# Neighbourhood attention with query tiles moved by half a block, one-bank score tiles and one transposed tile

## The chip, the cores and the metric

One core of a Trainium2 chip runs the whole program. The metric is device time in microseconds, from the runs of the program on that core; lower is better. Line numbers (L2205) are those of the kernel before.

## The reference, cut to what matters

The program is a stack of four transformer layers on 512 tokens. The last of them mixes tokens by neighbourhood attention, and only that layer is concerned here. The 512 latent tokens form a grid of 8 rows and 64 columns; 256 context tokens are keys as well. A query in column c sees all 8 rows of the 16 columns from clip(c - 8, 0, 48) on, and all 256 context keys:

```python
q, k, v, z = split(u @ w_in)           # 32 heads of 64; q and k are normalised
win_start = clip(cols - 8, 0, 48)
s = q . k_band * scale + rpb[row difference, column difference]
s = where(win_start <= kc < win_start + 16, s, -inf)
p = softmax(concat([s, q . k_ctx * scale]))
out = (p_band @ v_band + p_ctx @ v_ctx) * silu(z) @ w_out
```

## The kernel before, in words

Tokens are stored column by column (`grid_order`), 8 rows to a column, so 128 tokens are 16 grid columns and a query sees 128 consecutive keys. The layer (`second`, L1620, with L = 3) works in eight groups of four heads. While the attention of group g runs, the projections of group g+1 (q, k, v) and the gate z of group g are computed beside it as *pieces*, 24 matmuls each, which a table (`fill`) puts into numbered steps. Matrix products are made in two parts: each operand is a high part (fp32r) and a remainder, so a product is three matmuls (`mm3`, L583 to L585); the weights are split by ScalarE (L277) and GpSimd (L278) from a buffer that SP loads (L264).

`na_run` (L2168) runs 128 units, one for each group, head h and query tile j of 128 tokens. Latent keys come in four blocks of 128. Tile j needs the blocks B0[j] to B0[j]+NB[j]-1, that is two blocks for the outer tiles (j = 0, 3) and three for the middle ones (j = 1, 2), and the two blocks of the context. A unit goes through these functions:

- `A` (L2194): scores in PSUM tile `s` of two banks, of which there is **one** (`s.psum(3, 3, 0, 1)`, L1919): 256 or 384 latent columns and 256 context columns, each with KH and with KL (L2205, L2206). Rows 64 to 127 of KH and KL are copies of rows 0 to 63 made by a transfer on GpSimd's queue (`dup_now`, L1803). For j = 1, `bias` loads the next head's position bias (192 KB, L2190, on SP) and GpSimd adds it to three masks (L2192).
- `B` (L2208): VectorE adds mask and bias and takes the row maximum in one pass (L2221).
- `E` (L2224): ScalarE's exponential out of PSUM into P with the row sum.
- `Dm` (L2228): VectorE scales P by the reciprocal of the sum (L2231, L2232).
- `T` (L2234): TensorE transposes P's blocks (L2244) into two PSUM tiles, latent and context; ScalarE copies each as the high part (`pth`, `pch`; L411), VectorE subtracts for the remainder (`ptl`, `pcl`; L414).
- `G` (L2248), once per head: values times the transposed probabilities, four matmuls of 512 columns for the context (L2253) and two for each latent block over the two or three query tiles that see it (L2259). ScalarE moves half of the result (L2261), VectorE adds the other (L2262).
- `Y` (L2264): GpSimd multiplies by the gate, SP stores.

The order in a step i is written out by hand at the end of `na_run` (L2271 on): scores of unit i, deferred work (`s.due`), the first half of the step's piece, B of unit i, G if a head is complete, T of unit i-1, E of unit i, the rest of the piece, further pieces, Dm of unit i. Each engine runs its instructions in that order. `stack` (L1775) transposes the projected q and k and writes QS (high part in rows 0 to 63, remainder in rows 64 to 127) and KH, KL; its remainders are deferred by a step (`low`).

Of the kernel before, what the change touches and what calls it, by code (L numbers as in the profile page):

```python
# [161 lines left out]
def pack_cst():  # L162
# [11 lines left out]
    cols = np.arange(64)  # L174
    ws = np.clip(cols - 8, 0, 48)
    na = []
    for cb, b0, nb in ((0, 0, 2), (1, 0, 3), (3, 2, 2)):
        qc = cb * 16 + np.arange(128) // 8
        kc = b0 * 16 + np.arange(nb * 128) // 8
        ok = (kc[None, :] >= ws[qc][:, None]) & (kc[None, :] < ws[qc][:, None] + 16)  # L180
        na.append(np.where(ok, 0.0, NEG))
# [8 lines left out]
             ("cos", tok(cos)), ("sin", tok(sin * sgn)), ("mask", mask), ("na", np.concatenate(na, axis=1))]  # L190
    o = 0
# [11 lines left out]
def pack_rpb(i):  # L203
    rpb = i["b_rpb_2"][0]
    q = np.arange(128)
    qc, r = q // 8, q % 8
    k = np.arange(384)
    kc, kr = k // 8 - 16, k % 8
    a = kr[None, :] - r[:, None] + 7
    b = np.clip(kc[None, :] - qc[:, None] + 15, 0, 30)  # L210
    return np.ascontiguousarray(rpb[:, a, b])
# [89 lines left out]
class Next:  # L301
    """Normalised input of a layer, feature-major in two parts, filled a pair of token tiles at a time."""
# [76 lines left out]
class Net:  # L379
# [207 lines left out]
    def tm(s, ps, units, xh, xl, tok, n, ks=range(8)):  # L587
        """Eight blocks of a token-major product, or those of ks."""
# [6 lines left out]
    def fmm(s, ps, units, xh, xl, tok, n, c0=0, m=128, ks=range(8)):  # L595
        """The same with the features on the partitions."""
# [14 lines left out]
    def rows_gemm(s, keys, lhs, evac, tail, npair, flush, wide_first=False, mid=None, k_first=False):  # L611
        """Token-major product over four 256-column chunks; the last two go pair of tiles by pair of tiles."""
# [23 lines left out]
        def pair(i, c, us, free, between):  # L636
            """Two tiles, one weight unit after the other; the first unit is given back early where it is free."""
# [69 lines left out]
    def causal(s, units, qk, scale, mask, vs, pt, out, P, tmp, ofs, wide, fill, extra=lambda t: None):  # L707
        """Causal attention over (head, query tile) units; fill[t] holds the pieces of other work run in step t."""
# [368 lines left out]
    def out_proj(s, name, order, lhs, M, ssp, rowt, sqp, make, gain, part=None, late=None):  # L1077
        """part: the first chunk's sum over the first unit, already formed."""
# [502 lines left out]
    def tables2(s, pool, tmp):  # L1581
        """Rotary tables with the head gains folded in, the difference's factor and the output gain."""
# [37 lines left out]
    def second(s, L, nx):  # L1620
# [20 lines left out]
        QS = gp.tile([128, 4, qw], F32R, name="QS")  # L1641
# [114 lines left out]
        def gates_at(ts, g, chunks):  # L1756
            """z / (1 + exp(-z)), 128 columns at a time."""
# [17 lines left out]
        def stack(n, pr, tiles):  # L1775
            gain = None if diff else s.p("b" + n)
            c = slice(tiles[0] * 128, tiles[-1] * 128 + 128)
# [9 lines left out]
            def low():  # L1787
                for t in range(2):
# [130 lines left out]
        s.psum(*(2, 2, 0, 2) if diff else (3, 3, 0, 1))  # L1919
# [248 lines left out]
    def na_run(s, c):  # L2168
        nc, io, X = s.nc, s.io, s.X
        QS, KH, KL, SZ, V, yd = c.QS, c.KH, c.KL, c.SZ, c.V, c.yd  # L2170
        gp = s.pool("nag")
        na = gp.tile([128, 896], F32, name="na")
# [3 lines left out]
        WO = ((0, 512, 256), (1536, 1152, 1792))  # L2176
        pth, ptl = [gp.tile([128, 12, 128], F32R, name=n) for n in ("pth", "ptl")]
        pch, pcl = [gp.tile([128, 2, 512], F32R, name=n) for n in ("pch", "pcl")]
        B0 = (0, 0, 1, 2)
        NB = (2, 3, 3, 2)  # L2180
        rpb = X[0][:, 640:1024]
        P = [X[0][:, :640], X[1][:, :640]]
# [4 lines left out]
        def bias(h):  # L2187
            if h > 31:
                return
            nc.sync.dma_start(rpb, io["rpb"][h])  # L2190
            for o, a, c, w in zip(WO[h % 2], (128, 0, 0), (0, 256, 640), (256, 384, 256)):
                nc.gpsimd.tensor_tensor(bm[:, o:o + w], na[:, c:c + w], rpb[:, a:a + w], OP.add)  # L2192

        def A(u):  # L2194
# [3 lines left out]
            ps = s.s2.tile([128, 1024], F32, name="s2")  # L2198
            q = QS[:, h, j * 128:(j + 1) * 128]
            w = NB[j] * 128  # L2200
            k0 = B0[j] * 128
            c = 256 if h % 2 else 512
            x = d[u] = {"s": ps[:, 256:512 + w] if h % 2 else ps[:, 512 - w:768]}
            for o, kk in ((ps[:, 512:512 + w] if h % 2 else ps[:, 512 - w:512], slice(k0, k0 + w)), (ps[:, c:c + 256], slice(512, 768))):
                nc.tensor.matmul(o, q, KH[:, h, kk], start=True, stop=False)  # L2205
                nc.tensor.matmul(o, q, KL[:, h, kk], start=False, stop=True)  # L2206

        def B(u, i):  # L2208
            g, h, j = u
            x = d[u]  # L2210
            S = x["s"]
            w = S.shape[-1]
            o = WO[h % 2][(0, 1, 1, 2)[j]]
            if j in (1, 2):
                t = bm[:, 896:1536] if h % 2 else bm[:, o:o + w]
            else:
                a, b = (896, o) if h % 2 else (o, 896)
                t = bass.AP(tensor=bm.tensor, offset=bm.offset + a, ap=[bm.ap[0], [b - a, 2], [1, 256]])
                S = S.rearrange("p (a b) -> p a b", b=256)
            x["nb"], x["sm"] = [s.sml.tile([128, 1], F32, name=f"na_{k}") for k in ("nb", "s")]  # L2220
            nc.vector.tensor_tensor_reduce(S, S, t, -1.0, 3e38, OP.add, OP.min, x["nb"])  # L2221
            x["P"] = P[i % 2][:, :w]
# [11 lines left out]
        def T(u):  # L2234
            g, h, j = u
            x = d.pop(u)
            n = NB[j]
            b = 2 * B0[j] + j + 1
            sl = slice(b, b + 2 * n - 1, 2)
            q = slice(j * 128, (j + 1) * 128)  # L2240
            for k0, m, H, Lo in ((2 * (h % 2), n, pth[:, sl], ptl[:, sl]), (n * (1 - h % 2), 2, pch[:, :, q], pcl[:, :, q])):
                t = s.tp.tile([128, 4, 128], F32, name="tp")
                for k in range(m):
                    nc.tensor.transpose(t[:, k], x["P"][:, (k0 + k) * 128:(k0 + k + 1) * 128], s.ident)  # L2244
                s.act(H, t[:, :m], AF.Copy)
                s.sub_lo(Lo, t[:, :m], H)

        def G(g, h):  # L2248
            ps = s.mm.tile([128, 512], F32, name="mm")
            VS = V[g]  # L2250
            for k in range(2):
                for w, t in enumerate((pch, pcl)):
                    nc.tensor.matmul(ps, VS[:, 4 + k, h], t[:, k], start=k == 0 and w == 0, stop=False)  # L2253
            for k in range(4):
                c0, c1 = max(0, k - 1), min(3, k + 1)
                b = 2 * k + c0 + 1
                n = c1 - c0 + 1
# [67 lines left out]
```

## Time and profile before

| | |
|---|---|
| three runs | 3265.22, 3266.62, 3267.99 us |
| median | 3266.62 us |
| span of the profiled execution | 3260.0 us |
| instructions | 59267 |
| busy share PE, PEld, DVE, ACT, POOL | 95, 89, 66, 50, 47% |
| stretch of the 128 units | about 2473 to 3192 us of the span |

The profiled execution shows its span, from the first to the last instruction; a run's time has some microseconds around it, here 6.6 to the median. PE is TensorE's matmuls, PEld its weight loads, DVE VectorE, ACT ScalarE, POOL GpSimd, SP the queue of transfers. A matmul's shown duration includes a modelled end that overlaps the next one, so the price of a matmul in a stream is the distance from its start to the next start.

### The profile page before, as it was taken

Reading aid. Unit: us, or ns where it says so; the run is one execution under the profiler, and the core shown is the slowest. Engines: PE = TensorE matmul, PEld = TensorE weight load, DVE = VectorE, ACT = ScalarE, POOL = GpSimd, SP = SyncE. Lnnn points to the kernel's source line nnn. Section 1 sums busy time; section 2 is a strip of 40 time slices with the busy share of each in tenths; the row PEclk is TensorE's granted clock in tenths of the full one; section 3 lists DMA queues with packets and bytes.
Section 4 is the critical chain, followed back from the end, with each engine's and each line's share of the span. In section 5 each row is a group of like instructions: output and inputs, shape, how many; then the busy total and the mean of one; then the engine's idle time right before and its main releaser. Section 6 shows DMA issues by size and latency. Waiting matters only on the chain.

```text
span 3260.0 us, 59267 instructions
## 1 busy us (share of the span) xinstructions
PE 3097.0 (95%) x23124; PEld 2910.2 (89%) x23124; DVE 2143.7 (66%) x4332; ACT 1626.6 (50%) x3923; POOL 1527.3 (47%) x1344
## 2 busy tenths in 40 slices
PE   7999999998899999999999999998999999999889
PEld 7888889887788889889999999988999999999888
DVE  4885434466865354657777777778446777777775
ACT  4544533345765333455555555555235565555552
POOL 3433344434333444474654465443354554545544
PEclk9999999999999999999999999999999999999999
DMA  3122334432123343331222222212422323222324
GB/s 120 59 72 74 108 123 143 136 99 85 36 85 111 123 135 125 116 98 50 63 60 62 61 66 58 69 53 87 152 87 78 88 79 84 78 71 79 90 87 136
DMA packets 91012, 292.30 MB, mean 90 GB/s; under 512 B 18142, under 2 KB 23390, under 8 KB 87660
## 3 DMA queue, kind: packets, MB, share of 16 engines
q1 hardware_dynamic: 84028, 259.33, 24.7%
q0 software_dynamic: 5120, 25.17, 3.6%
q10 hardware_dynamic: 1584, 4.00, 0.4%
q8 instruction: 183, 3.00, 0.4%
q14 instruction: 97, 0.79, 0.1%
HBM read 244.38 MB, written 18.92 MB: 81 GB/s over the span
## 4 chain that ended last, share of the span: by engine, by line
PE 49%; DVE 11%; ACT 5%; issue 4%; POOL 3%; DMA 2%; SPq 0%; POOLq 0%; DVEq 0%; ACTq 0%
PE mm L583 12%; PE mm L585 12%; PE mm L584 12%; PE mm L2102 2%; ACT X L411 2%; POOL w_lo L278 2%; DMA KL<-KL 1%; PE s L2205 1%; PE tp L2244 1%; PE tp L2089 1%; PE mm L2259 1%; DVE s L2052 1%; PE mm L2253 1%; PE s L2206 1%; DVE X L735 1%
## 5 line engine op out<-in xcount | busy, mean ns | idle before, releaser
L278 POOL TENSOR_TENSOR w_lo<-w_raw,w_hi 128x1024 fp32r<-128x1024 f32 (+2 forms) x350 | 880.6, 2520 | 1033.8 <-ACT w_hi L277 1007.8
L583 PE MATMUL mm<-w_hi,hh 128*128 128x256 f32 (+3 forms) x2880 | 836.8, 291 | 7.8 <-ACT w_hi L277 2.5
L584 PE MATMUL mm<-w_lo,hh 128*128 128x256 f32 (+3 forms) x2880 | 817.0, 284 | 11.8 <-POOL w_lo L278 11.7
L585 PE MATMUL mm<-w_hi,hl 128*128 128x256 f32 (+3 forms) x2880 | 818.6, 284 | 2.8 <-POOL hl L414 2.4
L584 PEld LDWEIGHTS mm<-w_lo,hh 128*128 128x128 f32 x2880 | 548.0, 190 | 15.7 <-POOL w_lo L278 14.4
L583 PEld LDWEIGHTS mm<-w_hi,hh 128*128 128x128 f32 x2880 | 547.4, 190 | 16.0 <-ACT df_sq L411 8.5
L585 PEld LDWEIGHTS mm<-w_hi,hl 128*128 128x128 f32 x2880 | 546.2, 190 | 6.4 <-POOL hl L414 5.5
L277 ACT CAST w_hi<-w_raw 128x1024 fp32r<-128x1024 f32 (+2 forms) x355 | 366.5, 1036 | 206.0 <-PE mm L585 171.2
L583 PE MATMUL mm<-hh,w_hi 128*128 128x256 f32 (+1 forms) x1408 | 455.4, 323 | 3.0 <-DVE M L1088 2.8
L584 PE MATMUL mm<-hl,w_hi 128*128 128x256 f32 (+1 forms) x1408 | 448.2, 318 | 0.6
L585 PE MATMUL mm<-hh,w_lo 128*128 128x256 f32 (+1 forms) x1408 | 447.1, 318 | 1.2 <-DVE w_lo L278 1.2
L583 PEld LDWEIGHTS mm<-hh,w_hi 128*128 128x128 f32 x1408 | 266.0, 189 | 29.8 <-issue 5.2
L584 PE MATMUL mm<-w_lo,gh 128*128 128x256 f32 x1024 | 287.1, 280 | 1.4 <-POOL w_lo L278 1.4
L583 PE MATMUL mm<-w_hi,gh 128*128 128x256 f32 x1024 | 287.6, 281 | 0.0
L585 PE MATMUL mm<-w_hi,gl 128*128 128x256 f32 x1024 | 287.1, 280 | 0.1
L585 PEld LDWEIGHTS mm<-hh,w_lo 128*128 128x128 f32 x1408 | 265.7, 189 | 22.0 <-DVE w_lo L278 1.6
L584 PEld LDWEIGHTS mm<-hl,w_hi 128*128 128x128 f32 x1408 | 266.1, 189 | 21.3 <-DVE hl L345 1.7
L1267 DVE SCALAR_TENSOR_TENSOR macc<-modw,cg,macc 128x1024 f32<-128x1024 f32 x84 | 201.3, 2440 | 29.2 <-DMA modw<-in_mod 29.2
L584 PEld LDWEIGHTS mm<-w_lo,gh 128*128 128x128 f32 x1024 | 193.0, 188 | 1.9 <-POOL w_lo L278 1.6
L583 PEld LDWEIGHTS mm<-w_hi,gh 128*128 128x128 f32 x1024 | 193.2, 189 | 0.4
L585 PEld LDWEIGHTS mm<-w_hi,gl 128*128 128x128 f32 x1024 | 193.0, 188 | 0.5 <-DVE gl L414 0.5
L414 DVE TENSOR_TENSOR gl<-rsq,gh 128x512 fp32r<-128x512 f32 x64 | 45.6, 712 | 220.6 <-ACT gh L411 220.6
(372 smaller groups left out, 7089.0 us busy)
## 6 DMA issues: line engine op xcount, KB each, us to landing
w_raw<-in_w SPq DMA_DIRECT2D x336, 512.0 KB, 3.5
modw<-in_mod SPq DMA_DIRECT2D x24, 1024.0 KB, 5.8
KH<-KH POOLq DMA_DIRECT2D x32, 384.0 KB, 4.0
KL<-KL POOLq DMA_DIRECT2D x32, 384.0 KB, 5.0
xs<-X SPq DMA_DIRECT2D x12, 512.0 KB, 3.6
X<-xs SPq DMA_DIRECT2D x12, 512.0 KB, 6.7
yd<-ob SPq DMA_DIRECT2D x16, 384.0 KB, 2.3
X<-in_rpb SPq DMA_DIRECT2D x32, 192.0 KB, 3.7
```

The costliest lines, as they stand in the source:

```text
L277: nc.scalar.copy(hi[:, :m], raw[:, :m])
L278: (eng or nc.gpsimd).tensor_tensor(lo[:, :m], raw[:, :m], hi.bitcast(F32)[:, :m], OP.subtract)
L411: return s.nc.scalar.activation(out, in_, func, bias=bias, scale=scale, **kw)
L414: (eng or s.nc.vector).tensor_tensor(lo, x, hi.bitcast(F32), OP.subtract)
L583: mm(ps, ah, bh, start=first, stop=False)
L584: mm(ps, ah, bl, start=False, stop=False)
L585: mm(ps, al, bh, start=False, stop=last)
L735: nc.vector.tensor_scalar(d["P"][:, :d["n"]], d["P"][:, :d["n"]], rs, None, OP.mult)
L1267: nc.vector.scalar_tensor_tensor(acc[:, v], w[:, k2], cv, acc[:, v], OP.mult, OP.add)
L2052: nc.vector.tensor_tensor_reduce(S, S, s.zero.to_broadcast(list(S.shape)), nrq[:, h:h + 1], 3e38, OP.add, OP.min, nb)
L2089: nc.tensor.transpose(pt[:, k], ea[:, (k0 + k) * 128:(k0 + k + 1) * 128], s.ident)
L2102: nc.tensor.matmul(ps, x["w"][:, k], V[g][:, kb, p * 128:(p + 1) * 128], start=k == 0, stop=k == nk - 1)
```

## The change: what it does

Query tiles begin 64 tokens earlier: tile j covers tokens 128j - 64 to 128j + 63, and tile 0 holds the last 64 tokens and the first 64. Each tile then needs two latent blocks (tile 0: the first and the last), so scores are 512 columns wide in every unit. QS gets 64 columns in front that repeat its last 64 (a GpSimd copy). The mask is one of 256 columns for all inner tiles; for tile 0 the two quarters that no query sees are preset with -1e30 and the other two come by transfer. Score tiles are one bank, and there are two of them; keys are read through a view of two runs of columns (`seg`). The four transposes go to one PSUM tile with one copy and one subtraction. Values are multiplied over two query tiles per latent block, and the result is turned back by 64 tokens in the add. Lines that only shorten comments are left out.

```diff
@@ pack_cst
-    cols = np.arange(64)
-    ws = np.clip(cols - 8, 0, 48)
-    na = []
-    for cb, b0, nb in ((0, 0, 2), (1, 0, 3), (3, 2, 2)):
...
+    qc, kc = np.arange(128) // 8, np.arange(256) // 8
+    na = np.where((kc[None, :] >= qc[:, None]) & (kc[None, :] < qc[:, None] + 16), 0.0, NEG)
@@ second
-        QS = gp.tile([128, 4, qw], F32R, name="QS")
+        q0 = 0 if diff else 64
+        QS = gp.tile([128, 4, q0 + qw], F32R, name="QS")
@@ stack
-            c = slice(tiles[0] * 128, tiles[-1] * 128 + 128)
+            o = q0 if n == "q" else 0
+            c = slice(o + tiles[0] * 128, o + tiles[-1] * 128 + 128)
@@ stack, low
+                if n == "q" and not diff:
+                    nc.gpsimd.tensor_copy(QS[:, 2 * pr:2 * pr + 2, 0:64], QS[:, 2 * pr:2 * pr + 2, qw:qw + 64])
@@ second
-        s.psum(*(2, 2, 0, 2) if diff else (3, 3, 0, 1))
+        s.psum(*(2, 2, 0, 2) if diff else (3, 3, 0, 2))
@@ na_run
-        bm = gp.tile([128, 2048], F32, name="bm")
-        nc.vector.memset(bm[:, 896:1152], 0.0)
-        pth, ptl = [gp.tile([128, 12, 128], F32R, name=n) for n in ("pth", "ptl")]
-        pch, pcl = [gp.tile([128, 2, 512], F32R, name=n) for n in ("pch", "pcl")]
+        bm = [gp.tile([128, 3, 256], F32, name=f"bm{k}") for k in range(2)]
+        for t in bm:
+            nc.vector.memset(t[:, 2], 0.0)
+            nc.vector.memset(t[0:64, 0, 0:128], NEG)
+            nc.vector.memset(t[64:128, 0, 128:256], NEG)
+        pth, ptl = [gp.tile([128, 4, 4, 128], F32R, name=n) for n in ("pth", "ptl")]
@@ bias
-            nc.sync.dma_start(rpb, io["rpb"][h])
-            for o, a, c, w in zip(WO[h % 2], (128, 0, 0), (0, 256, 640), (256, 384, 256)):
-                nc.gpsimd.tensor_tensor(bm[:, o:o + w], na[:, c:c + w], rpb[:, a:a + w], OP.add)
+            t = bm[h % 2]
+            nc.sync.dma_start(rpb, io["rpb"][h, :, 0:256])
+            for a in (0, 64):
+                nc.sync.dma_start(t[a:a + 64, 0, 128 - 2 * a:256 - 2 * a], io["rpb"][h, a:a + 64, 256:384])
+            nc.gpsimd.tensor_tensor(t[:, 1], na, rpb, OP.add)
+        def seg(x, a, b, w):
+            return bass.AP(tensor=x.tensor, offset=x.offset + a, ap=[x.ap[0], [b - a, 2], [1, w]])
@@ A
-            ps = s.s2.tile([128, 1024], F32, name="s2")
...
-            for o, kk in ((ps[:, 512:512 + w] if h % 2 else ps[:, 512 - w:512], slice(k0, k0 + w)), (ps[:, c:c + 256], slice(512, 768))):
-                nc.tensor.matmul(o, q, KH[:, h, kk], start=True, stop=False)
-                nc.tensor.matmul(o, q, KL[:, h, kk], start=False, stop=True)
+            S = s.s2.tile([128, 512], F32, name="s2")
+            if j:
+                parts = [(S, lambda K: seg(K[:, h, :], 128 * j - 128, 512, 256))]
+            else:
+                parts = [(S[:, 0:256], lambda K: seg(K[:, h, :], 0, 384, 128)), (S[:, 256:512], lambda K: K[:, h, 512:768])]
+            for o, kk in parts:
+                nc.tensor.matmul(o, q, kk(KH), start=True, stop=False)
+                nc.tensor.matmul(o, q, kk(KL), start=False, stop=True)
@@ B
+            S = x["s"].rearrange("p (a b) -> p a b", b=256)
+            nc.vector.tensor_tensor_reduce(S, S, t[:, 1:3] if j else t[:, 0:3:2], -1.0, 3e38, OP.add, OP.min, x["nb"])
@@ T
-            for k0, m, H, Lo in ((2 * (h % 2), n, pth[:, sl], ptl[:, sl]), (n * (1 - h % 2), 2, pch[:, :, q], pcl[:, :, q])):
-                t = s.tp.tile([128, 4, 128], F32, name="tp")
-                for k in range(m):
-                    nc.tensor.transpose(t[:, k], x["P"][:, (k0 + k) * 128:(k0 + k + 1) * 128], s.ident)
-                s.act(H, t[:, :m], AF.Copy)
-                s.sub_lo(Lo, t[:, :m], H)
+            t = s.tp.tile([128, 4, 128], F32, name="tp")
+            for k in range(4):
+                nc.tensor.transpose(t[:, k], x["P"][:, k * 128:(k + 1) * 128], s.ident)
+            s.act(pth[:, j], t, AF.Copy)
+            s.sub_lo(ptl[:, j], t, pth[:, j])
@@ G
-                    nc.tensor.matmul(ps, VS[:, 4 + k, h], t[:, k], start=k == 0 and w == 0, stop=False)
+                    nc.tensor.matmul(ps.rearrange("p (a b) -> p a b", b=128), VS[:, 4 + k, h], t[:, :, 2 + k], start=k == 0 and w == 0, stop=False)
-                c0, c1 = max(0, k - 1), min(3, k + 1)
...
+                a, b = ((0, 0), (1, 0)) if k == 0 else ((0, 1), (3, 1)) if k == 3 else ((k, 1), (k + 1, 0))
                 for w, t in enumerate((pth, ptl)):
-                    nc.tensor.matmul(ps[:, c0 * 128:(c1 + 1) * 128], VS[:, k, h], t[:, b:b + n], start=False, stop=k == 3 and w == 1)
+                    f = t.rearrange("p a b n -> p (a b n)")
+                    nc.tensor.matmul(seg(ps, a[0] * 128, b[0] * 128, 128), VS[:, k, h], seg(f, (4 * a[0] + a[1]) * 128, (4 * b[0] + b[1]) * 128, 128), start=False, stop=k == 3 and w == 1)
-            s.defer(lambda: nc.vector.tensor_tensor(ofs[h // 2][hp:hp + 64], ps[0:64], tmp[0:64], OP.add))
+            def add():
+                o = ofs[h // 2]
+                for a, b in ((slice(0, 448), slice(64, 512)), (slice(448, 512), slice(0, 64))):
+                    nc.vector.tensor_tensor(o[hp:hp + 64, a], ps[0:64, b], tmp[0:64, b], OP.add)
+            s.defer(add)
```

## Rows read from the trace of the kernel before

**Rows 1.** The page: busy time and share of TensorE and VectorE over the span

```profile
PE 3097.0 (95%) x23124; PEld 2910.2 (89%) x23124; DVE 2143.7 (66%) x4332; ACT 1626.6 (50%) x3923; POOL 1527.3 (47%) x1344
```

**Rows 2.** Busy time by stretch: start:end, length, busy PE PEld DVE ACT POOL, clock, DMA share, GB/s

```profile
2648.00:2737.00 89.00, 86.07 (x683) 83.41 (x681) 67.90 (x154) 52.33 (x136) 45.66 (x46) 1.00 0.30 80
```

**Rows 3.** Waits in the stretch: us in total, times, longest; weight loads, then SP

```profile
PEld s L2205 <- ACT X L411: 39.2, 58, 3.3
PEld tp L2244 <- issue: 7.9, 4, 2.5
PEld s L2206 <- DMA KL<-KL: 5.1, 8, 1.6
...
PEld tp L2244 <- DVE X L2232: 1.7, 1, 1.7
...
SPq L264 <- POOL w_lo L278: 607.5, 62, 20.0
```

**Rows 4.** Timeline (start us, us, engine, line) of three places; [idle before <-releaser]

```profile
2592.71 0.19 PEld L2205 LDWEIGHTS s<-KH,QS 128*128 128x128 f32 x1 [0.48 <-ACT X L411]
2592.89 0.56 DVE L2232 TENSOR_SCALAR X<-X,na_r 128x640 f32<-128x640 f32 x1
2592.99 0.34 PE L2206 MATMUL s<-KL,QS 128*128 128x384 f32 x1
...
2654.59 2.43 POOL L278 TENSOR_TENSOR w_lo<-w_raw,w_hi 128x1024 fp32r<-128x1024 f32 x1 [6.68 <-ACT w_hi L277]
2655.29 2.02 DVE L2232 TENSOR_SCALAR X<-X,na_r 128x512 f32<-128x512 f32 x1
...
2667.81 0.19 PEld L2205 LDWEIGHTS s<-KH,QS 128*128 128x128 f32 x1 [1.48 <-ACT X L411]
2667.99 0.56 DVE L2232 TENSOR_SCALAR X<-X,na_r 128x640 f32<-128x640 f32 x1
2669.82 0.71 PE L2244 MATMUL tp<-ident,X 128*128 128x128 f32 x5
```

**Rows 5.** Timeline of TensorE: starts of matmuls that follow without a wait

```profile
2594.83 0.71 PE L2244 MATMUL tp<-ident,X 128*128 128x128 f32 x5
...
2837.40 0.39 PE L2253 MATMUL mm<-pcl,VS 128*128 128x512 f32 x1
2837.63 0.28 PE L2259 MATMUL mm<-pth,VS 128*128 128x256 f32 x1
2837.74 0.28 PE L2259 MATMUL mm<-ptl,VS 128*128 128x256 f32 x1
2837.86 0.33 PE L2259 MATMUL mm<-pth,VS 128*128 128x384 f32 x1
2838.03 0.34 PE L2259 MATMUL mm<-ptl,VS 128*128 128x384 f32 x1
...
2838.79 0.60 PE L2244 MATMUL tp<-ident,X 128*128 128x128 f32 x4
```

**Rows 6.** Groups by shape in the stretch: count | busy us, mean ns | idle before

```profile
L414 DVE TENSOR_TENSOR pcl<-tp,pch 128x256 fp32r<-128x256 f32 x128 | 52.9, 414 | 0.0
L2221 DVE CUSTOM_DVE_ANT_0 s<-s,bm 128x640 f32<-128x640 f32 x64 | 52.9, 827 | 0.9
L2221 DVE CUSTOM_DVE_ANT_1 s<-s,bm 128x512 f32<-128x512 f32 x64 | 44.3, 693 | 6.2 <-PE s L2206 5.8
L411 ACT ACTIVATE pch<-tp 128x256 fp32r<-128x256 f32 x128 | 48.5, 379 | 0.0
L414 DVE TENSOR_TENSOR ptl<-tp,pth 128x384 fp32r<-128x384 f32 x64 | 35.5, 555 | 28.1 <-ACT pth L411 28.1
L411 ACT ACTIVATE pth<-tp 128x384 fp32r<-128x384 f32 x64 | 31.5, 492 | 79.5 <-PE tp L2244 78.7
...
L2192 POOL TENSOR_TENSOR bm<-na,X 128x256 f32<-128x256 f32 x64 | 48.1, 751 | 119.0 <-DMA X<-in_rpb 110.9 <-PE s L2206 8.1
L2192 POOL TENSOR_TENSOR bm<-na,X 128x384 f32<-128x384 f32 x32 | 34.1, 1065 | 0.0
```

More of the change, by code (lines that the diff above doesn't have):

```diff
@@ L173, in pack_cst @@
     mask = np.concatenate([np.where(np.arange(512)[None, :] <= q + 128 * j, 0.0, NEG) for j in range(4)], axis=1)
-    cols = np.arange(64)
-    ws = np.clip(cols - 8, 0, 48)
-    na = []
-    for cb, b0, nb in ((0, 0, 2), (1, 0, 3), (3, 2, 2)):
[L178 to L181, printed above, removed]
+    qc, kc = np.arange(128) // 8, np.arange(256) // 8
+    na = np.where((kc[None, :] >= qc[:, None]) & (kc[None, :] < qc[:, None] + 16), 0.0, NEG)
     inv8 = (f32(500000.0) ** (-np.arange(0, 16, 2, dtype=f32) / f32(16))).astype(f32)
@@ L189, in pack_cst @@
     parts = [("ident", np.eye(128)), ("eps", eps), ("invr", invr), ("invc", invc), ("ph", ph), ("sg", sg),
-             ("cos", tok(cos)), ("sin", tok(sin * sgn)), ("mask", mask), ("na", np.concatenate(na, axis=1))]
+             ("cos", tok(cos)), ("sin", tok(sin * sgn)), ("mask", mask), ("na", na)]
     o = 0
@@ L205, in pack_rpb @@
     q = np.arange(128)
-    qc, r = q // 8, q % 8
     k = np.arange(384)
-    kc, kr = k // 8 - 16, k % 8
-    a = kr[None, :] - r[:, None] + 7
-    b = np.clip(kc[None, :] - qc[:, None] + 15, 0, 30)
+    a = (k % 8)[None, :] - (q % 8)[:, None] + 7
+    inner = (k // 8 - 8)[None, :] - (q // 8)[:, None]
+    outer = (k // 8 - 32)[None, :] - (q % 64 // 8 + np.where(q < 64, 8, 0))[:, None]
+    b = np.clip(np.where(k < 256, inner, outer) + 15, 0, 30)
     return np.ascontiguousarray(rpb[:, a, b])
@@ L2171, in na_run @@
         gp = s.pool("nag")
-        na = gp.tile([128, 896], F32, name="na")
+        na = gp.tile([128, 256], F32, name="na")
         nc.sync.dma_start(na, s.cst("na"))
-        bm = gp.tile([128, 2048], F32, name="bm")
-        nc.vector.memset(bm[:, 896:1152], 0.0)
-        WO = ((0, 512, 256), (1536, 1152, 1792))
-        pth, ptl = [gp.tile([128, 12, 128], F32R, name=n) for n in ("pth", "ptl")]
-        pch, pcl = [gp.tile([128, 2, 512], F32R, name=n) for n in ("pch", "pcl")]
[L2179 to L2182, printed above, removed]
+        bm = [gp.tile([128, 3, 256], F32, name=f"bm{k}") for k in range(2)]
[4 more added lines that the diff above has]
+        pth, ptl = [gp.tile([128, 4, 4, 128], F32R, name=n) for n in ("pth", "ptl")]
+        rpb = X[0][:, 640:896]
+        P = [X[0][:, :512], X[1][:, :512]]
         tmp = X[2][:, 0:512]
@@ L2197, in A @@
                 bias(4 * g + h + 1)
-            ps = s.s2.tile([128, 1024], F32, name="s2")
+            S = s.s2.tile([128, 512], F32, name="s2")
+            d[u] = {"s": S}
             q = QS[:, h, j * 128:(j + 1) * 128]
[L2200 to L2203, printed above, removed]
-            for o, kk in ((ps[:, 512:512 + w] if h % 2 else ps[:, 512 - w:512], slice(k0, k0 + w)), (ps[:, c:c + 256], slice(512, 768))):
-                nc.tensor.matmul(o, q, KH[:, h, kk], start=True, stop=False)
-                nc.tensor.matmul(o, q, KL[:, h, kk], start=False, stop=True)
+            if j:
[5 more added lines that the diff above has]
+                nc.tensor.matmul(o, q, kk(KL), start=False, stop=True)
         def B(u, i):
@@ L2210, in B @@
             x = d[u]
[L2211 to L2219, printed above, removed]
+            S = x["s"].rearrange("p (a b) -> p a b", b=256)
+            t = bm[h % 2]
             x["nb"], x["sm"] = [s.sml.tile([128, 1], F32, name=f"na_{k}") for k in ("nb", "s")]
-            nc.vector.tensor_tensor_reduce(S, S, t, -1.0, 3e38, OP.add, OP.min, x["nb"])
-            x["P"] = P[i % 2][:, :w]
+            nc.vector.tensor_tensor_reduce(S, S, t[:, 1:3] if j else t[:, 0:3:2], -1.0, 3e38, OP.add, OP.min, x["nb"])
+            x["P"] = P[i % 2]
         def E(u):
@@ L2251, in G @@
             for k in range(2):
-                for w, t in enumerate((pch, pcl)):
-                    nc.tensor.matmul(ps, VS[:, 4 + k, h], t[:, k], start=k == 0 and w == 0, stop=False)
+                for w, t in enumerate((pth, ptl)):
+                    nc.tensor.matmul(ps.rearrange("p (a b) -> p a b", b=128), VS[:, 4 + k, h], t[:, :, 2 + k], start=k == 0 and w == 0, stop=False)
             for k in range(4):
-                c0, c1 = max(0, k - 1), min(3, k + 1)
-                b = 2 * k + c0 + 1
-                n = c1 - c0 + 1
+                a, b = ((0, 0), (1, 0)) if k == 0 else ((0, 1), (3, 1)) if k == 3 else ((k, 1), (k + 1, 0))
                 for w, t in enumerate((pth, ptl)):
-                    nc.tensor.matmul(ps[:, c0 * 128:(c1 + 1) * 128], VS[:, k, h], t[:, b:b + n], start=False, stop=k == 3 and w == 1)
+                    f = t.rearrange("p a b n -> p (a b n)")
+                    nc.tensor.matmul(seg(ps, a[0] * 128, b[0] * 128, 128), VS[:, k, h], seg(f, (4 * a[0] + a[1]) * 128, (4 * b[0] + b[1]) * 128, 128), start=False, stop=k == 3 and w == 1)
             hp = (h % 2) * 64
             s.act(tmp[0:64], ps[64:128], AF.Copy)
-            s.defer(lambda: nc.vector.tensor_tensor(ofs[h // 2][hp:hp + 64], ps[0:64], tmp[0:64], OP.add))
+            def add():
[3 more added lines that the diff above has]
+            s.defer(add)
         def Y(g, j):
```

4 lines of the change are left out of this document (removed).

## The prediction

> **What bounds the kernel now.** I read the page's busy shares first: TensorE is busy 95% of the span and no other engine comes near it [rows 1]. So a change pays only where it shortens TensorE's own stream or a wait in that stream. Then I cut out the stretch of the neighbourhood attention (eight head groups of some 90 us) with the busy time by stretch: in a steady group VectorE is busy 68 of 89 us, ScalarE 52, GpSimd 46, and TensorE 86 [rows 2]. The rest of TensorE's time is in the waits of its weight loads: 39.2 us in 58 units go to the first score matmul waiting for ScalarE, 9.6 us to the transposes (7.9 put down to issue, 1.7 to the scaled P), 5.1 us to the copied half of KL [rows 3]. The 39.2 us is the one PSUM score buffer: the scores of a unit may not be written until the exponential of the unit before has read it. The last rows give the pitch of TensorE's stream, start to start, which is its true price since ends overlap: 0.23 us for 512 columns, 0.115 for 256, 0.17 for 384; a transpose is 0.11 (0.71 against 0.60 us for five and four) [rows 5].
>
> The sum is made against this execution: span 3260.0 us, 6.6 us under the median of the runs shown (3266.62). I take its differences off that median; two parts in a thousand do not change them.
>
> **The change part by part.**
>
> *Fewer score columns.* The two middle tiles of each head (64 units) read 384+256 key columns twice, 0.17+0.17+0.115+0.115 = 0.57 us. Now they read 512 twice, 0.466. That is 0.11 us a unit, 7 us. Outer tiles keep 512 columns; fewer, longer matmuls are worth nothing, as two 256 cost as much as one 512 [rows 5].
>
> *Fewer value columns.* Per head eight latent matmuls go from four of 256 and four of 384 columns to eight of 256: 4 x 0.057 = 0.23 us, times 32 heads 7.3 us. The four context matmuls of 512 stay.
>
> *One transpose fewer* in those 64 units: 64 x 0.11 = 7.0 us. These three, 21.4 us, are TensorE's own time and are lost only if the new operand shapes run slower (rivals).
>
> *Two score buffers.* The wait on the exponential goes, and what is late next is the transposes' wait for the scaled probabilities (Dm, then T). I checked the slack. In a usual unit the scores start at 2592.71 after 0.48 us of wait, VectorE ends the scaling at 2593.45, and the transposes start at 2594.83: 1.38 us to spare, so that wait vanishes whole [rows 4, 5]. Once a group there is a long one: 1.48 us before the start at 2667.81, scaling over at 2668.55, transposes at 2669.82, 1.27 us to spare [rows 4]. The unit before it has a usual wait as well (0.48), so TensorE would come 1.9 us sooner, more than the slack by 0.6; add some 1.1 us of column savings in those steps, and take off the 1 us that VectorE gains over these two or three units (next item): about 0.7 us is left as a new wait at the transposes, 5 us over seven groups. In the last group some units have no other product beside them; the longest wait there is 3.3 us [rows 3], its chain is exposed, and I leave about 4 us standing. So 39.2 - 5 - 4 = 30 us. After a wait the second score matmul also starts late (0.28 us instead of 0.17 [rows 4]); without the wait most of that goes: 58 x 0.05 = 3 us.
>
> *VectorE and ScalarE.* The masking pass goes from 827 to 693 ns in the 64 middle units; two remainders (555+414 ns) become one over 512 columns, which must lie between 0.55 and 0.97 us, by the slope of the two rows 0.69; two copies (492+379 ns) become one, between 0.49 and 0.87, by slope 0.60 [rows 6]. VectorE gains 0.13+0.28 = 0.41 us in a middle unit and 0.15 in an outer one, some 36 us in all. It is off the path except in the stretch just costed, so it counts only there. The single copy must wait for all four transposes, where the first of two began after two: 0.2 us later, against 0.1 to 0.3 us less to copy; zero. The output add gets a second instruction over 64 columns: between nothing and the 0.69 us of the masking pass over 512 columns [rows 6], I take 0.15, times 32, under VectorE's idle time.
>
> *GpSimd and SP.* The bias adds fall from two of 256 (751 ns) and one of 384 (1065 ns) per head to one of 256: 1.8 us, times 32, 58 us off GpSimd [rows 6]. Sixteen copies of 128 x 128 come in, each between nothing and 0.75 us (the 256-column add), I take 0.4. A copy waits for VectorE's low part of QS, and GpSimd's weight remainders, bias adds and the KH/KL transfers stand behind it; but it is issued three or more units before those queries are read. SP gets 64 more transfers of 32 KB. SP's queue mostly stands waiting for GpSimd to give back a weight buffer (607.5 us [rows 3]); the new transfers are needed three units later. Both at zero; if that cover went, the masking pass of a head's first tile would wait.
>
> *What moves for the worse.* At each group's first unit TensorE waits for the KL transfer; it will arrive 0.1 us earlier there, seven times: 1 us. The memsets lie in the prologue beside that same transfer: zero.
>
> Sum: 21.4 + 30 + 3 - 1 = 53 us, so 3266.6 - 53 = **3213 us**.
>
> [...] The new value matmuls of key block 3 write output columns 0-127 and 384-511, two runs apart; no row before has such an output. I price them as contiguous, 0.115 us. [...]
>
> **The rivals.**
>
> 1. *The wait only moves.* Scores start early, then TensorE stands at the transposes for VectorE, all 39.2 us of it. For: transposes already wait 9.6 us [rows 3]. Against: the slack of 1.27 to 1.38 us [rows 4, 5] and VectorE's load of 68 in 89 us [rows 2]. Only the columns are left: 3266.6 - 21.4 + 1 = 3246. Two buffers that still serialise would give the same time. Chance 0.13.
>
> 2. *More than forecast.* GpSimd and VectorE hold each other up: a scaling pass took 2.02 us where others of its kind take 0.5 (0.56 at 640 columns), and ended as GpSimd's 2.43 us instruction ended [rows 4]. With 58 us less on GpSimd the waits at the transposes go too: 39.2 + 3 + 21.4 + 9.6 = 73, 3193. Chance 0.11.
>
> 3. *Slower.* The moving operand of nearly all new matmuls comes in two or four separate runs of columns (keys plus context; probability blocks 512 apart). No matmul before reads so. If a split operand streamed at half rate, the price is 96 units x 2 x 512, 32 x 2 x 256 and 32 heads x 4096 columns, 246 thousand in all, at 0.233 us per 512: 112 us, so 3325. It decides from 1.5 times the contiguous price on, where it eats the 53. Against: VectorE's masking pass on two separate runs costs 693 ns for 512 and the contiguous one 827 for 640, the same per column [rows 6]; runs of 128 leave few jumps. Chance 0.05.
>
> 4. *Split outputs only.* The 64 matmuls with output in two runs at twice the price: 64 x 0.115 = 7 us, 3220. Chance 0.05; this is the rule above.
>
> The forecast itself has 0.66.
>
> **How the numbers follow.** About 0.2% (6.5 us) is what a measurement of this kernel tells from no change. The forecast's own range is 3199 to 3229: the recovered wait between half and all of 39.2 us (10 us more, 9 us less) and some 5 us either way for the unpriced operations. Rivals 2 and 4 lie in 3192 to 3240, with the forecast 0.82; rivals 1 and 3 are left out. Slower is rival 3, 0.05; the tail of rival 1, with the copies or transfers uncovered, gives 0.03 to "same"; the rest, 0.92, is faster.
>
> **What would show it.** In the profile after: per group some 83 us instead of 89 to 90; the wait of the score matmuls on ScalarE gone or a few us; the transposes' wait for the scaled probabilities (na_r, X) grown from 9.6 to no more than about 20 us, mostly in the first units of a group and in the last group; score matmuls of 512 columns 0.23 us apart; the two split-output matmuls 0.115 apart; GpSimd in the stretch some 50 us less busy. It is wrong if the transposes wait 40 us (rival 1), if 512-column matmuls stand more than 0.3 us apart (rival 3), or if a wait on QS, bm or KL of over 5 us appears.

## The result, and the profile after

The changed kernel takes 3222.34 us (median of four runs, 3220.53 to 3223.91) against 3267.30 for the kernel before (four runs, 3265.22 to 3268.20). The ratio is 0.9862 with a 95% interval of 0.9848 to 0.9875. That is 45 us less where 53 were forecast; 3222 lies inside the range of 3192 to 3240. Lines of code are now those of the kernel after: scores L2212 (with KH) and L2213 (with KL), transposes L2239, values L2249 and L2254, the scaling of P L2232, remainders L409, ScalarE's copies and exponentials L406, the weight split L272 (ScalarE) and L273 (GpSimd).

The first part of the page, as in [rows 1]:

```profile
PE 3067.4 (95%) x22868; PEld 2882.8 (89%) x22868; DVE 2132.6 (66%) x4241; ACT 1605.0 (50%) x3795; POOL 1473.9 (46%) x1296
```

TensorE lost 30 us of busy time and kept its share of 95%. GpSimd lost 53 us. VectorE lost only 11, although its instructions became shorter by far more; that is the first sign of what follows.

One whole head group (the third of eight, from its first score matmul to that of the next group), by the busy time by stretch, columns as in [rows 2]:

```profile
2633.10:2719.40 86.30, 81.98 (x655) 79.37 (x654) 68.88 (x143) 49.94 (x121) 39.28 (x40) 1.00 0.31 83
```

A steady group took 89.4 to 89.8 us and now takes 84.5 to 86.3 (77.4 in the first, 87.5 in the last); some 83 were forecast. TensorE is idle 4.3 us in this group. The waits of the weight loads in the stretch (columns as in [rows 3]: us in total, times, longest):

```profile
PEld tp L2239 <- issue: 23.3, 16, 3.1
PEld s L2213 <- DMA KL<-KL: 7.1, 8, 1.6
PEld tp L2239 <- DVE X L2232: 5.0, 4, 3.9
PEld tp L2239 <- PE mm L579: 3.2, 3, 1.1
...
PEld tp L2239 <- PE mm L2254: 0.5, 1, 0.5
```

The same waits seen on the matmuls name the releaser where the weight load says "issue":

```profile
PE tp L2239 <- DVE X L2232: 27.5, 22, 3.5
```

The 39.2 us for the score buffer [rows 3] is gone whole. The four rows of the transposes add up to 32.0 us, where they were 9.6: 22 us came back as a wait for VectorE's scaled P. The wait for KL grew by 2 us.

An account from the starts of successive matmuls in the stretch, each against its contiguous price of [rows 5], agrees. TensorE's own work went from 626.6 to 605.6 us. The wait ahead of the first score matmul went from 40.8 to 2.1, the delay of the second from 16.6 to 11.3, the wait at the transposes from 10.2 to 32.2, and the small delays among the projections' products rose by 5.5. Together that is 37.5 us less; from the first score matmul to the last transpose the two profiled executions differ by 36.8, and their spans by 38.7 (3260.0 and 3221.3). The medians differ by 45 because the profiled execution of before was a quick one: after, time and span differ by 1.84 us (3223.14 and 3221.3), which puts that execution of before some 5 us under its median. The 6.6 us that the section on the kernel before takes for the time around an execution are mostly this.

The 5.5 us come nearly whole from TensorE's granted clock. Between the first score matmul and the last transposes it stood at 0.50 of full for 25 us after and 10 us before, in several pieces. One of them, as in [rows 2], and two products in it:

```profile
2824.14:2827.55 3.41, 3.41 (x16) 3.22 (x16) 3.03 (x8) 1.33 (x4) 2.40 (x4) 0.50 1.07 284
```

```profile
2824.69 0.41 PE L579 MATMUL mm<-w_lo,hh 128*128 128x256 f32 x1
2824.91 0.41 PE L580 MATMUL mm<-w_hi,hl 128*128 128x256 f32 x1
```

A product of 256 columns takes 0.21 to 0.22 us there, start to start, and 0.12 outside. The products' delays within these pieces are 7.7 us after and 2.6 before, 5.1 of the 5.5. In the fifth to seventh groups a piece begins 0.6 to 1.3 us after TensorE has stood about 2 us at the transposes; in the second to fourth the same wait was followed by none.

The groups by shape, as in [rows 6]:

```profile
L2232 DVE TENSOR_SCALAR X<-X,na_r 128x512 f32<-128x512 f32 x128 | 112.2, 877 | 4.6
L409 DVE TENSOR_TENSOR ptl<-tp,pth 128x512 fp32r<-128x512 f32 x128 | 88.2, 689 | 93.4 <-ACT pth L406 93.3
L2221 DVE CUSTOM_DVE_ANT_0 s<-s,bm 128x512 f32<-128x512 f32 x96 | 66.4, 692 | 2.3 <-PE s L2213 1.2
...
L2261 DVE TENSOR_TENSOR X<-mm,X 64x64 f32<-64x64 f32 x32 | 6.6, 206 | 0.0
...
L406 ACT ACTIVATE pth<-tp 128x512 fp32r<-128x512 f32 x128 | 76.5, 598 | 117.7 <-PE tp L2239 116.9
...
L1793 POOL CAST QS<-QS 128x128 fp32r<-128x128 f32 x14 | 4.1, 292 | 26.4 <-DVE QS L1791 26.4
```

The merged remainder takes 0.689 us (estimated 0.69), the merged copy 0.598 (0.60), the masking pass 0.692 everywhere. The added pieces cost 0.206 us (the second output add, taken as 0.15) and 0.292 us (the copy of QS, taken as 0.4). The odd row is the scaling: its mean is 877 ns while its shortest is 485 ns.

TensorE's stream at a head's values and at a unit's scores, from the timeline:

```profile
2643.68 0.40 PE L2249 MATMUL mm<-pth,VS 128*128 128x512 f32 x1
2643.91 0.40 PE L2249 MATMUL mm<-ptl,VS 128*128 128x512 f32 x1
...
2645.29 0.28 PE L2254 MATMUL mm<-pth,VS 128*128 128x256 f32 x1
2645.40 0.28 PE L2254 MATMUL mm<-ptl,VS 128*128 128x256 f32 x1
2645.52 0.60 PE L2239 MATMUL tp<-ident,X 128*128 128x128 f32 x4
...
2653.48 0.40 PE L2212 MATMUL s<-KH,QS 128*128 128x512 f32 x1
...
2653.72 0.39 PE L2213 MATMUL s<-KL,QS 128*128 128x512 f32 x1
```

L2249 reads four separate runs of columns and the scores read two: 0.23 and 0.24 us to the next start, as for 512 contiguous columns [rows 5]. The last two L2254 are those of key block 3 with output in two runs: 0.11 and 0.12 us, as for 256 contiguous columns.

The largest regular wait at the transposes is 2.1 us at the second unit of each of six groups, the second to the seventh (12.7 us in all). For the third group the timeline shows how it comes about:

```profile
2646.96 0.69 ACT L406 ACTIVATE X<-s,na_nb 128x512 f32<-128x512 f32 x1
...
2647.64 1.04 ACT L272 CAST w_hi<-w_raw 128x1024 fp32r<-128x1024 f32 x1
...
2647.83 0.95 DVE L1765 RECIPROCAL ge<-ge 128x128 f32<-128x128 f32 x1
...
2648.81 2.37 POOL L273 TENSOR_TENSOR w_lo<-w_raw,w_hi 128x1024 fp32r<-128x1024 f32 x1 [1.41 <-ACT w_hi L272]
2648.84 2.62 DVE L2232 TENSOR_SCALAR X<-X,na_r 128x512 f32<-128x512 f32 x1
...
2651.61 0.63 PE L2239 MATMUL tp<-ident,X 128*128 128x128 f32 x4 [1.95 <-DVE X L2232]
```

ScalarE ends the unit's exponential and at once makes the high part of a weight tile; VectorE is meanwhile in a gate reciprocal. Both are through within 0.1 us of each other, and GpSimd's subtraction starts 0.03 us before the scaling (0.03 to 0.08 us in four of the six groups, 0.3 in two). The scaling then takes 2.62 us instead of 0.49 and ends 0.28 us after GpSimd does; TensorE stands at the transposes. So here an instruction of GpSimd that had begun held the scaling until it was through; all 43 of the 128 scalings that take over 0.75 us end so, 0.28 to 0.29 us after one.

### The profile page after: what moved, and what is told of

Same layout as the page of the kernel before. It is cut to its first block, busy times and chain, and to the rows that moved or that the text cites. A ratio compares the mean times of both kernels' runs of the same rounds, so it can differ in the third digit from the quotient of the medians.

```text
span 3221.3 us, 58548 instructions
## 1 busy us (share of the span) xinstructions
PE 3067.4 (95%) x22868; PEld 2882.8 (89%) x22868; DVE 2132.6 (66%) x4241; ACT 1605.0 (50%) x3795; POOL 1473.9 (46%) x1296
## 4 chain that ended last, share of the span: by engine, by line
PE 49%; DVE 13%; ACT 4%; issue 4%; DMA 3%; POOL 2%; SPq 0%; POOLq 0%; DVEq 0%; ACTq 0%
PE mm L578 13%; PE mm L580 12%; PE mm L579 12%; PE mm L2101 3%; DMA KL<-KL 1%; POOL w_lo L273 1%; PE tp L2239 1%; ACT X L406 1%; PE tp L2088 1%; DVE s L2051 1%; PE mm L2254 1%; PE mm L2249 1%; DVE X L2232 1%; PE s L2040 1%; DVE ge L1765 1%
## 5 line engine op out<-in xcount | busy, mean ns | idle before, releaser
L273 POOL TENSOR_TENSOR w_lo<-w_raw,w_hi 128x1024 fp32r<-128x1024 f32 (+2 forms) x350 | 879.0, 2517 | 1019.7 <-ACT w_hi L272 994.5
L579 PE MATMUL mm<-w_lo,hh 128*128 128x256 f32 (+3 forms) x2880 | 820.3, 285 | 11.3 <-POOL w_lo L273 11.3
L272 ACT CAST w_hi<-w_raw 128x1024 fp32r<-128x1024 f32 (+2 forms) x355 | 366.1, 1035 | 206.0 <-PE mm L580 171.3
L409 DVE TENSOR_TENSOR gl<-rsq,gh 128x512 fp32r<-128x512 f32 x64 | 45.6, 713 | 220.4 <-ACT gh L406 220.4
```

The source lines that it names most:

```text
L272: nc.scalar.copy(hi[:, :m], raw[:, :m])
L273: (eng or nc.gpsimd).tensor_tensor(lo[:, :m], raw[:, :m], hi.bitcast(F32)[:, :m], OP.subtract)
L409: (eng or s.nc.vector).tensor_tensor(lo, x, hi.bitcast(F32), OP.subtract)
L579: mm(ps, ah, bl, start=False, stop=False)
```

## The experiments

All but the last but one start from the kernel after; ratios are to the kernel before, timed beside it on the same chip. Two theories stood at the start: **hold** (the wait left at the transposes is the scaling held behind GpSimd's weight subtraction) and **load** (VectorE's chain is simply too long once the scores come early).

**One score buffer again.** This parts the shorter operands from the second buffer.

```diff
-        s.psum(*(2, 2, 0, 2) if diff else (3, 3, 0, 2))
+        s.psum(*(2, 2, 0, 2) if diff else (3, 3, 0, 1))
```

> The changed kernel with one score buffer in place of two, all else as changed. My theory (the columns and the transpose are worth 21 us by themselves, the second buffer the rest): the score matmuls wait for the exponential again, 35 to 40 us, the transposes wait about 10 us as before, and the time is about 3246 us, 0.993 of the kernel before. The rival (the shorter masking, copying and subtracting passes shorten the chain, so that one buffer would nearly do): score waits under 20 us and about 3230 us.

Measured: 3250.71 us, ratio 0.9942 (0.9925 to 0.9958).

```profile
PEld s L2212 <- ACT X L406: 36.3, 55, 2.9
PEld tp L2239 <- issue: 17.4, 10, 2.5
```

The column part alone is worth 0.0058 of 3267, some 19 us (14 to 25 by the interval), and the second buffer the rest of the way from 0.9942 to 0.9862, 26 us. The score wait is back at 36.3 us, so it is the second buffer that removed it. With one buffer the transposes already wait 19.1 us (17.4 and 1.7 for the scaled P) where some 10 were expected: 1.8 us at the second unit of six groups, where the kernel before had that wait in two. So nearly half of the growth from 9.6 to 32.0 us came without the second buffer.

**The weight split after the scaling, in the second step of each group.** The split is the same work; only its place in the step moves.

```diff
-            s.W.tick()
+            if r != 1:
+                s.W.tick()
...
                 Dm(u[0])
+            if r == 1:
+                s.W.tick()
```

> The changed kernel, with the weight split (ScalarE's cast and GpSimd's subtraction) of the second step of each group issued after that unit's scaling and not before it. My theory (in that unit VectorE's scaling starts 0.03 to 0.3 us after a GpSimd subtraction of 2.4 us and is held until it ends, so the transposes wait 2.1 us): the scaling of that unit takes 0.5 us, the wait at the transposes falls by about 2 us in each of six groups, 12 us in all, and the time is about 3210 us. The rival (VectorE is simply too full at the start of a group): no change, 3219 to 3225 us.

Measured: 3207.86 us, ratio 0.9811 (0.9791 to 0.9831), against 0.9862 (0.9848 to 0.9875). The place shown above, now:

```profile
2650.08 0.49 DVE L2232 TENSOR_SCALAR X<-X,na_r 128x512 f32<-128x512 f32 x1
...
2650.72 0.62 PE L2239 MATMUL tp<-ident,X 128*128 128x128 f32 x4
2650.84 2.42 POOL L273 TENSOR_TENSOR w_lo<-w_raw,w_hi 128x1024 fp32r<-128x1024 f32 x1
```

```profile
PEld tp L2239 <- issue: 10.8, 12, 3.2
...
PEld tp L2239 <- PE mm L579: 4.5, 6, 0.8
PEld tp L2239 <- DVE X L2232: 4.4, 4, 3.2
...
PEld tp L2239 <- PE mm L2254: 0.5, 1, 0.5
```

The scaling takes 0.49 us and the transposes wait for nothing there. Their wait fell from 32.0 to 20.2 us and the second to seventh groups now take 82.3 to 83.7 us, the 83 of the forecast. All six waits of 2.1 us are gone: the hold is confirmed by its removal. The place of one split in a step is worth some 17 us: 12 are the wait, and some 4 the clock, which stood at 0.50 for 10 us in place of 25 (mean over the profiled execution 0.991 against 0.989) and stayed at 1.00 in the second to sixth groups.

**The scaling with an operand in PSUM.** The scaling is written as an operation with the score tile in PSUM as an unused second operand; its result is the same.

```diff
-            nc.vector.tensor_scalar(x["P"], x["P"], r, None, OP.mult)
+            nc.vector.scalar_tensor_tensor(x["P"], x["P"], r, x["s"], OP.mult, OP.bypass)
```

> The changed kernel, with the scaling of P written as an operation of VectorE that takes the score tile in PSUM as a second operand and does not use it, in place of the one with a single operand in SBUF. My theory (the single-operand scaling in SBUF is what GpSimd can hold up): each scaling takes about 0.7 us, never 2; the waits at the transposes fall from 32 to about 10 us; about 3200 us. The rival (VectorE's load is what counts): 128 times 0.2 us more work on VectorE, 3224 to 3230 us.

Measured: 3214.57 us, ratio 0.9834 (0.9814 to 0.9855). That misses the expectation by 15 us.

```profile
L2232 DVE SCALAR_TENSOR_TENSOR X<-X,na_r,s x128: 746/748/750, 2475.4 to 3136.0; 128x512 f32<-128x512 f32 x128
```

```profile
2647.61 2.41 POOL L273 TENSOR_TENSOR w_lo<-w_raw,w_hi 128x1024 fp32r<-128x1024 f32 x1 [0.84 <-ACT w_hi L272]
...
2647.90 0.75 DVE L2232 SCALAR_TENSOR_TENSOR X<-X,na_r,s 128x512 f32<-128x512 f32 x1
```

The row gives the shortest, median and longest duration in ns: all 128 lie within 746 to 750, and at the same place the scaling runs beside the subtraction. So in this kernel the hold depends on where the operands lie, not on the engines as such: with all of them in SBUF a scaling took up to 2.62 us, with one in PSUM 0.75. It is not the kind of operation either: the kernel after has SCALAR_TENSOR_TENSOR with both operands in SBUF (L427, 16 and 24 columns), and all 14 of them in the stretch take 2.4 us beside the subtraction, where the same line takes 0.18 us (24 columns) in an earlier layer with no GpSimd instruction beside it. But each scaling is 0.26 us longer than a free one, and the transposes still wait 26.5 us, now in smaller pieces (0.25 to 0.6 us at the second unit, 0.9 at the third, 1.1 at the twelfth). That speaks for a share of the load theory: the chain of exponential, reciprocal, scaling and transposes has no slack at those units, so more work on VectorE shows up at TensorE. It is not shown in full: at the twelfth unit the wait grew from 0.4 to 1.1 us, more than the 0.26 us of one scaling.

**GpSimd's relief taken back.** Two more adds of GpSimd per head, on scratch data, stand in for the bias adds that the change removed.

```diff
...
             nc.gpsimd.tensor_tensor(t[:, 1], na, rpb, OP.add)
+            for w in (384, 256):
+                nc.gpsimd.tensor_tensor(scr[:, 0:w], wide[:, 0:w], wide[:, 384:384 + w], OP.add)
```

> The changed kernel with two more GpSimd adds per head, of 384 and 256 columns on scratch tiles, so that GpSimd does as much for the bias as before the change: 1.8 us more, 58 us over the 32 heads. If GpSimd's relief is part of the gain (more scalings held up, weight remainders later): 5 to 15 us slower than the changed kernel, 3227 to 3237 us. If GpSimd's load is covered: 3219 to 3225 us.

Measured: 3227.88 us, ratio 0.9873 (0.9853 to 0.9894), which can't be told from 0.9862. The time alone would lie in the first range, but the kernel before, timed beside it, was also 3.6 us slower than beside the kernel after. GpSimd's busy time is back at 1527.1 us, as before [rows 1], and the transposes wait 28.9 us, 3 less than after. Less work on GpSimd was worth some 4 us by the ratios, which is within their noise: how long it is busy mattered little here, when its long instructions start mattered much.

**All splits late.** The edit of the second experiment in every step.

> The changed kernel with the weight split issued after the unit's scaling in every step, not only in the second of each group. My theory (the scalings that are held up are those that start after a GpSimd weight subtraction of their own step): fewer than 20 of the 128 scalings are held up, against 43, the transposes wait under 15 us, and the time is 0.979 to 0.981 of the kernel before. Rivals: the subtraction of one step then meets the scaling of the next, so that as many are held up (0.984 or more); or weights come late and the products wait for them (over 3 us of waits on w_lo).

Measured: 3206.57 us, ratio 0.9813 (0.9798 to 0.9829). The wait at the transposes fell to 13.4 us, yet the time did not move against 0.9811. Two things were not as expected. Of 128 scalings 45 are still over 0.75 us (43 after), against fewer than 20 expected: the subtraction of one step now meets the scaling of the next, as the first rival had it, but most of these fall where TensorE has slack, so the time did not rise to the rival's 0.984. No wait on w_lo showed, which puts the second rival out. And a new wait came in at the first unit of the last group:

```profile
PEld s L2212 <- POOL QS L1793: 4.5, 1, 4.5
```

```profile
3043.83 2.40 POOL L273 TENSOR_TENSOR w_lo<-w_raw,w_hi 128x1024 fp32r<-128x1024 f32 x1
3046.17 0.57 POOL L1802 DMA_DIRECT2D KH<-KH  x1
...
3053.28 0.55 PE L2212 MATMUL s<-KH,QS 128*128 128x256 f32 x1 [4.26 <-DMA KH<-KH]
```

The profile puts the weight load's wait down to the copy of QS, but that copy (3052.41) belongs to the group's other two heads. What ended last is the transfer of KH: issued by GpSimd behind the late split, 7.0 us to its landing, 3053.1.

**Late only where it pays.** Late in the second step of each group, in step 14 of the seventh group and in all of the last.

```diff
+            late = r == 1 or g == 6 and r == 14 or g == 7
...
```

> The changed kernel with the split issued after the scaling in the second step of each group, in step 14 of the seventh group and in every step of the last group: the places where a held-up scaling ended in a wait of the transposes. My theory: of the 20 us of waits that the late split of the second step left, the 3.1 us of the seventh group go and 4 to 6 us of the last group's 8.7; 0.978 to 0.980 of the kernel before, 6 to 9 us under that run. The rival (these waits are VectorE's load and the length of the chain): 0.981.

Measured: 3210.41 us, ratio 0.9821 (0.9805 to 0.9837): no gain over the second experiment, where 6 to 9 us were expected. The transposes wait 14.1 us, but the same 4.5 us at the last group's first unit is there, since the split of step 14 is one that stands ahead of that transfer; and TensorE waits 3.5 us for a remainder made by GpSimd (hl), 2.0 in the second experiment.

**The copy of QS on VectorE.**

```diff
-                    nc.gpsimd.tensor_copy(QS[:, 2 * pr:2 * pr + 2, 0:64], QS[:, 2 * pr:2 * pr + 2, qw:qw + 64])
+                    nc.vector.tensor_copy(QS[:, 2 * pr:2 * pr + 2, 0:64], QS[:, 2 * pr:2 * pr + 2, qw:qw + 64])
```

> The changed kernel with the copy of QS's 64 columns on VectorE and not on GpSimd. GpSimd's queue stood 26 us for VectorE before these copies; if nothing that matters stands behind them, as I held, the time stays within 3 us of the changed kernel, 0.985 to 0.987. The rival (the copies delay the weight remainders and the KL transfers behind them): waits on KL at the groups' first units fall from 12.6 to under 9 us and the time by 4 us or more.

Measured: 3226.50 us, ratio 0.9870 (0.9851 to 0.9889), no difference. GpSimd's 26.4 us of waiting for QS were hidden, as the prediction held, and the weight loads' wait on KL is 6.6 us against 7.1. (The 12.6 us of the expectation add this wait of the weight loads to that of the matmuls behind them, 5.5 us, which is the same time.) The run is of use for something else. In most groups the second unit lost its race as after, but in the fifth group it went the other way:

```profile
2827.27 0.69 DVE L2232 TENSOR_SCALAR X<-X,na_r 128x512 f32<-128x512 f32 x1
2827.62 2.58 POOL L273 TENSOR_TENSOR w_lo<-w_raw,w_hi 128x1024 fp32r<-128x1024 f32 x1
```

Here the scaling is ahead of the subtraction by 0.35 us, takes 0.69 (a shorter GpSimd instruction, the bias add from 2826.94 to 2827.67, holds it), and TensorE waits 0.2 us; in the group before it GpSimd was ahead by 0.03 us (2741.77 and 2741.80), the scaling took 2.60, and TensorE waited 2.1.

**The late split in the kernel before.** The edit of the second experiment, made to the kernel before.

> The kernel before, with the split of the second step of each group issued after the scaling. My theory (before, TensorE stood for the score buffer and so came to the transposes late; a held-up scaling showed in only two of the seven groups there): 2 to 5 us faster than before, 0.998 to 0.9995. The rival (the hold-up cost before what it costs after): 12 us or more, 0.996 or less.

Measured: 3263.31 us (12 runs), ratio 0.9984 (0.9975 to 0.9993), 5 us.

```profile
PEld s L2205 <- ACT X L411: 39.1, 58, 3.3
...
PEld tp L2244 <- issue: 4.3, 2, 2.5
...
PEld tp L2244 <- DVE X L2232: 2.2, 2, 1.7
```

The transposes' wait fell from 9.6 to 6.5 us, the two waits of 1.8 us at second units are gone, and the score wait stayed; what else is in the 5 us was not traced. The hold was there before too (41 of 128 scalings over 0.75 us), but TensorE, held up at the scores, came to the transposes too late to see most of it.

**All late but at the last seam.** All splits late except in the last three steps of the seventh group, at the seam to the last group.

```diff
+            late = not (g == 6 and r >= 13)
...
```

> Weight splits issued after the scaling in all steps except the last three of the seventh group (where the late split held up the GpSimd copy of QS and the KH transfer for unit 112). Theory (the 4.5 us wait at unit 112 is those three late splits, nothing else): it goes back under 0.5 us, the transposes wait 13.7 + up to 3.2 us (the unit before 112 may lose its race again), so 1.5 to 4.5 us less than with all splits late: ratio 0.979 to 0.981, about 3203 us. Rival (the copy is late because GpSimd's whole queue is later by then): the wait at unit 112 stays over 3 us and the time is that of all splits late, 0.981 to 0.982.

Measured: 3206.33 us, ratio 0.9800 (0.9785 to 0.9816).

The transposes wait 13.7 us. The timeline at the seam:

```profile
3038.60 2.34 POOL L273 TENSOR_TENSOR w_lo<-w_raw,w_hi 128x1024 fp32r<-128x1024 f32 x1 [2.03 <-ACT w_hi L272]
3039.56 1.66 DVE L2232 TENSOR_SCALAR X<-X,na_r 128x512 f32<-128x512 f32 x1
3041.37 1.09 PE L2239 MATMUL tp<-ident,X 128*128 128x128 f32 x4 [2.96 <-DVE X L2232]
3041.90 0.57 POOL L1802 DMA_DIRECT2D KH<-KH  x1
...
3048.09 0.19 PEld L2212 LDWEIGHTS s<-KH,QS 128*128 128x128 f32 x1 [0.21 <-issue]
```

The split goes out early, the unit there loses its race again (3.1 us), KH is issued and lands in 6.1 us, just in time: 0.2 us instead of 4.5. So the late split ahead of KH was the cause. In time the step is too small to be told from all splits late (intervals overlap); against the kernel after it is clear: 0.9800 (0.9785 to 0.9816) and 0.9862 (0.9848 to 0.9875), some 20 us. The four versions with late splits (0.9811, 0.9813, 0.9821, 0.9800) all beat both kernels.

## Why the prediction was right, and what it missed

It was right in sign and range because the bound was right: TensorE's stream and one named wait. That 45 us come so near to 53 is in part luck: the sum was made against the execution with the span of 3260.0 us, and against that one the fall is 38.7 us, 14 less than the sum. Point by point:

- **Columns and transposes, 21.4 us.** Right: TensorE's own work fell by 21.0 in the stretch. With one buffer alone the kernel gained 19, but the transposes wait 9.5 us longer there, so that run does not confirm the figure by itself.
- **Score wait.** That all 39.2 us go is right. That 30 of them are kept was **mis-sized**: the wait at the transposes was to grow by 9 us, to about 19, and grew by 22, to 32.0. So 17 were kept. The failing step is "about 0.7 us is left as a new wait at the transposes, 5 us over seven groups": the first seven groups hold 22.7 us of waits, the last 9.5. The slack was read from places where a scaling took its 0.56 us; the prediction had the row of a scaling held for 2.02 us in its hands [rows 4] and used it only for rival 2, as a gain to be had from less work on GpSimd, not as a cost that appears when TensorE comes sooner. Some 9.5 of the 22 us are there with one buffer, so they do not come from the score wait's end but from the other parts of the change. The second experiment shows that the splits in the second steps account for 12 us of the 32, the fifth and ninth that splits ahead of the scaling account for some 18. The 14 us that remain in the ninth (0.7 to 1.4 at the third unit of most groups, 3.1 at the seam, 4.3 in the last group) were not taken apart further.
- **Second score matmul, 3 us, and KL, 1 us the other way.** The delay behind the first score matmul, KL's included, fell by 5.3 us where 2 net were forecast; KL alone rose by 2.
- **Not in the sum:** 5.5 us of small delays among the projections' products, 5.1 of them in the time at the lower clock (25 us of it against 10). The second experiment, without the long waits, has 10 us of it again.
- **VectorE 36 us lighter:** 11 by the page. The passes named did become 36 us shorter (8.6 the masking, 27.3 the remainders). Against that the scalings grew from 99.4 to 112.2 us, since the time over 0.5 us of the held ones went from 32.4 to 48.6, and the output add in two parts costs 4.5 us more than in one (4.8 taken: the second part 6.6, the first 2.1 less). The shown durations fall by 17 us in all; the page counts time in which two overlap once.
- **GpSimd and SP at zero.** Right: the copy on another engine changed nothing, and GpSimd's 53 us less were worth some 4, within the noise.
- **Rival 1** is true for more than half of the wait, not for all of it: 22 of 39. **Rival 2** had the mechanism and the wrong lever: not less work on GpSimd but another order. Its size, 3193, was not reached; with the order changed the kernel stands at some 3206. **Rival 3** is out: split moving operands run at 0.23 to 0.24 us for 512. **Rival 4** is out: 0.11 and 0.12 us with output in two runs. The doubled price was an assumption that no run shows: output in two runs of 128 columns costs what 256 contiguous columns do, 0.115 us [rows 5].
- **The signs.** The transposes were to wait no more than about 20 us and wait 32.0, so that sign failed. A wait on KL of over 5 us was to speak against the forecast, but it was 5.1 us before the change already; 7.1 after tells little.

## What to carry to other kernels

When a wait on the bounding engine is removed, ask what its next wait is with the durations that rows show at that very place, stalls included, not with an instruction's usual duration. A scaling of VectorE from SBUF to SBUF did not end here until a GpSimd instruction that had begun before it was through (2.62 us in place of 0.49), so on a chain without slack issue GpSimd's long work after it, and check that no transfer queued on GpSimd slips behind that work (4.5 us at the last seam). Here 0.03 us in the order of issue was worth 2.1 us at a unit, so before changing work try changing its place in the step.

## What the runs showed of the hardware that was not expected

- All 43 held scalings of the kernel after end 0.28 to 0.29 us after a GpSimd instruction, whenever they began: 2.62 us when one starts 0.03 us behind. A lead of 0.02 us is not enough: in eight units the product with the gate begins 0.02 us behind the scaling and still holds it. With a lead of 0.08 us the scaling takes its 0.49 us, and it is the gate's product that takes 0.72 in place of 0.46 us:

```profile
2626.36 0.49 DVE L2232 TENSOR_SCALAR X<-X,na_r 128x512 f32<-128x512 f32 x1
2626.45 0.72 POOL L1766 TENSOR_TENSOR SZ<-SZ,ge 128x128 f32<-128x128 f32 x1 [0.60 <-DVE na_r L2231]
...
2632.47 0.76 DVE L2232 TENSOR_SCALAR X<-X,na_r 128x512 f32<-128x512 f32 x1
2632.49 0.46 POOL L1766 TENSOR_TENSOR SZ<-SZ,ge 128x128 f32<-128x128 f32 x1 [0.60 <-DVE na_r L2231]
```

- With a PSUM tile as second operand the scaling takes 0.75 us and was never held, in 128 cases.
- Splitting a matmul's moving operand into two or four runs of columns, or its PSUM output into two, had no price that the pitch shows (0.23 to 0.24 us for 512 columns, 0.11 to 0.12 for 256).
- A transfer of 64 partitions of KH from GpSimd's queue took 6.1 and 7.0 us from issue to landing at the last seam (KH and KL: 3.5 to 7.3 in the kernel after), so a split of 2.4 us ahead of it was enough to cost 4.3.
